# Where the feed-forward's side sums stand: pair 0's sums directly behind their products, w_down's sums two half steps later, the copies of w_down on their own

## The chip, the cores and the metric

The kernel runs on one core of one Trainium2 chip. A core has five engines with a queue of instructions each: TensorE (PE: matmuls, and PEld for the loading of their weights), VectorE (DVE), ScalarE (ACT), GpSimd (POOL) and SyncE (SP, which here only starts DMAs). An engine takes its own instructions strictly in order and waits for others through semaphores. The metric is the device time of one execution in microseconds; lower is better.

## The reference

One layer of a streaming encoder on 1024 tokens of width 1024, float32: token mixing, cross-attention into 256 memory tokens, and a SwiGLU feed-forward (FFN) with a hidden width of 2816. The part that matters here is the last:

```python
def swiglu(h, w_gate, w_up, w_down):
    return (jax.nn.silu(h @ w_gate) * (h @ w_up)) @ w_down
...
        h = rms_norm(x, ffn_pre_g)
        x = x + rms_norm(swiglu(h, w_gate, w_up, w_down), ffn_post_g)
```

## The kernel before

Every product is made of three matmuls, in a split form: an operand `x` is kept as a rounded part (`hi`, by ScalarE, line 113) and a remainder (`lo`, by VectorE, line 115), and `hi*hi + hi*lo + lo*hi` is accumulated in PSUM.

The FFN multiplies blocks by a scheme of Strassen's kind, with seven products in place of eight. The hidden width is cut into 22 tiles of 128, taken as 11 **pairs** (`NPAIR`), and each pair has two **half steps**: m = 0 for w_gate, m = 1 for w_up. A half step is written (pair, m) below. In each:

- `operands(i, m)` (line 1405 on) loads the pair's two weight tiles (L1409), makes the sums S1 to S4 of their blocks (L1417 on GpSimd; L1415 on VectorE for the first), and splits six or seven operands (`op`). `made[0]` remembers the last of GpSimd's sums. It is called one half step ahead.
- `gate_up(i, m, ...)` issues the seven products (each 12 matmuls, `product`, L1314) into four banks of PSUM: `p1`, S4, S3, `p2`, T2, T4, T1. Bank 1 and bank 3 are used twice: ScalarE copies what the first product left (`keep`, L1330) before TensorE adds the second. `add` (L1335) is VectorE's addition of a bank to a copy; the first one in a half step makes `u2`. What is in `held` is issued behind `u2`.
- `sums` makes the four result blocks, c11, c21, c12 and `p7` (L1335, L1460). For m = 0 ScalarE puts Silu on each (L1466). For m = 1 `finish_hid` multiplies the blocks with them (L1357) and stores three of the four to `hs_d` (L1362), a tensor in DRAM. Then, for every pair but pair 0, `hid_sums(i)` makes four more sums of the finished blocks, S3, S1, S2 and S4 (L1372, VectorE), and stores them too.

Pair 0 is special. Its w_gate half is done by eight plain products, and its w_up half, (0, 1), is written out by hand between `operands(0, 1, dve)` and `sums(0, 1, ...)`. Its `hid_sums(0)` is not called there: it is put into `held` of the next half step, (1, 0), behind `u2` and that half step's held operands.

The second matrix, w_down, is needed in blocks and in sums of blocks, too. `wd_sums(k)`, for k = 0 to 21, does two things for half of pair k // 2: it copies one or two blocks of w_down from DRAM to DRAM (`wd_d`, L1380; each behind a certain read of `x1` in the cross-attention, by `issue_after`), and it loads the blocks into the one buffer `wt` (L1383), makes four sums in place on GpSimd (L1387) and stores them to `wt_d` (L1388). The GpSimd part is put behind `made[0]`. It is called at the end of each half step, and twice more at the end.

Then seven **down** products (`DOWN`) read chunks of two pairs from `hs_d` and `wd_d` or `wt_d` into buffers `slab` (L1527, L1529), split them and multiply (L1608). The first takes "11" and `wd_d`, the second S2 and `wt_d`. There are 16 `slab` buffers, which the FFN's own operands occupy first.

The order in each queue is not the order of the text. A planner simulates the kernel when it is built and takes, for each engine, the instruction that is ready in its simulated time and stands earliest in the text; `issue_after(x)` adds an order behind `x` on the same engine. Buffers of a pool are handed on as they come free: 13 for `ev`, 10 for `op`, 1 for `wt`.

Of the kernel before, what the change touches and what calls it, by code (L numbers as in the profile page):

```python
# [52 lines left out]
def layer(ctx: ExitStack, tc: tile.TileContext, a, out):  # L53
# [15 lines left out]
    def slab(shape, dt=F32R):  # L69
        return slabp.tile(shape, dt, name="slab", tag="slab")  # L70
# [1239 lines left out]
    def product(ps, w, name, first):  # L1310
        (wh, wl), (bh, bl) = w, hB[name]
        for k in range(4):
            for n, (x, y) in enumerate(((wh, bh), (wh, bl), (wl, bh))):
                pe.matmul(ps, x[:, k], y[:, k], start=first and k + n == 0, stop=k == 3 and n == 2,  # L1314
                          skip_group_check=not first)
# [28 lines left out]
    def ev():  # L1344
        return evp.tile([P, 512], F32, name="ev", tag="ev")

    def plain_product(f, t):
        ps = (g_ps if t else x_ps)([P, 512])
        for n, name in enumerate((("11", "21"), ("12", "22"))[t]):
            product(ps, plain[0, f][n], name, n == 0)  # L1350
        hid[f, t] = ev()
        with tc.issue_after(tail[0].ins):
            act.activation(out=hid[f, t], in_=ps, func=AF.Silu)

    def finish_hid(i, f, t, u):
        h = hid[f, t]
        dve.tensor_tensor(out=h, in0=u, in1=h, op=ALU.mult)  # L1357
        if (f, t) != (0, 1):
            hid_store(i, "%d%d" % (t + 1, f + 1), h)

    def hid_store(i, name, t):
        stC.dma_start(out=hs_d[HID.index(name), i], in_=t)  # L1362

    def hid_sums(i):

        a11, a12, a21, a22 = hid.pop((0, 0)), hid.pop((1, 0)), hid.pop((0, 1)), hid.pop((1, 1))
        t = {}
        for name, x, y, fn in (("S3", a11, a21, ALU.subtract), ("S1", a21, a22, ALU.add),
                               ("S2", "S1", a11, ALU.subtract), ("S4", a12, "S2", ALU.subtract)):
            t[name] = ev()  # L1370
            x, y = (t[v] if isinstance(v, str) else v for v in (x, y))
            dve.tensor_tensor(out=t[name], in0=x, in1=y, op=fn)  # L1372
            hid_store(i, name, t[name])

    def wd_sums(k):

        p, cs = k // 2, slice(k % 2 * 256, k % 2 * 256 + 256)
        for f, h in ((0, 0), (1, 0), (1, 1))[2 * (k % 2):2 + k % 2]:
            with tc.issue_after(x1_read[min(3 + k // 4, 7)].ins):
                sp.dma_start(out=wd_d[f, h, p], in_=a["w_down"][2 * p + f][:, h * 512:h * 512 + 512])  # L1380
        w = wtp.tile([P, 2, 2, 256], F32, name="wt", tag="wt")
        for f in range(2):
            sp.dma_start(out=w[:, f], in_=a["w_down"][2 * p + f].rearrange("p (h c) -> p h c", c=512)[:, :, cs])  # L1383
        b11, b12, b21, b22 = w[:, 0, 0], w[:, 0, 1], w[:, 1, 0], w[:, 1, 1]
        with tc.issue_after(made[0].ins) if made[0] else ExitStack():
            for o, x, y in ((b11, b12, b11), (b12, b22, b12), (b22, b22, b11), (b21, b21, b22)):
                pool.tensor_tensor(out=o, in0=x, in1=y, op=ALU.subtract)  # L1387
            stC.dma_start(out=wt_d[p, :, :, :, cs], in_=w)  # L1388
# [11 lines left out]
    def op(src):  # L1400
        o = opp.tile([P, 2, 4, P], F32R, name="op", tag="op")
        split(o[:, 0], o[:, 1], src)
        return o[:, 0], o[:, 1]

    def operands(i, m, engine=None, held=None):

        rw = slab([P, 2, KT, P], F32)
        for f in range(2):
            sp.dma_start(out=rw[:, f].rearrange("p k f -> p (k f)"), in_=a[GU[m]][2 * i + f])  # L1409
        a11, a12, a21, a22 = rw[:, 0, 0:4], rw[:, 0, 4:8], rw[:, 1, 0:4], rw[:, 1, 4:8]  # L1410
        s2, s3, s4 = (ssp.tile([P, 4, P], F32, name="ss", tag="ss") for _ in range(3))
        s1 = a21
        def sub(o, x, y, fn=ALU.subtract):
            if engine:
                engine.tensor_tensor(out=o, in0=x, in1=y, op=fn)  # L1415
            else:
                made[0] = pool.tensor_tensor(out=o, in0=x, in1=y, op=fn)  # L1417
        o = {"11": op(a11)} if i else {}
        sub(s3, a11, a21)
        if held is None:  # L1420
            o["S3"] = op(s3)
        sub(s1, a21, a22, ALU.add)
        sub(s2, s1, a11)
        sub(s4, a12, s2)

        def rest():
            if held is not None:
                o["S3"] = op(s3)
            o["S4"] = op(s4)
            if i:  # L1430
                o["12"] = op(a12)
            o["S2"] = op(s2)
            o["22"] = op(a22)
            o["S1"] = op(s1)
        if held is None:
            rest()
        else:
            held.append(rest)
        return o

    def gate_up(i, m, w, q, held=()):
        q.p1(w["11"])
        p1 = q.keep(1)
        product(q.bank(4), w["S4"], "22", True)
        product(q.bank(3), w["S3"], "T3", True)
        p7 = q.keep(3)
        q.p2(w["12"])
        product(q.bank(2), w["S2"], "T2", True)
        u2 = q.add(2, p1)
        with tc.issue_after(q.added.ins) if held else ExitStack():  # L1450
            for part in held:
                part()
        product(q.bank(3), w["22"], "T4", False)
        product(q.bank(2), w["S1"], "T1", False)
        sums(i, m, q, p1, p7, u2, q.b[1])

    def sums(i, m, q, p1, p7, u2, c11):
        c21 = q.add(3, u2, False)
        u4 = q.add(2, p1, False)
        dve.tensor_tensor(out=p7, in0=u4, in1=p7, op=ALU.add)  # L1460
        c12 = q.add(4, u4, False)
        c = {(0, 0): c11, (0, 1): c12, (1, 0): c21, (1, 1): p7}
        if m == 0:
            for k, t in c.items():
                hid[k] = ev() if k == (0, 0) else t
                act.activation(out=hid[k], in_=t, func=AF.Silu)  # L1466
        else:
            for (f, t), u in c.items():
                finish_hid(i, f, t, u)
            if i:  # L1470
                hid_sums(i)

    seq = [(i, m) for i in range(1, NPAIR) for m in range(2)]
    ws = {}
# [4 lines left out]
    second = x_ps([P, 512])  # L1479
    product(second, plain[1, 0][1], "21", True)  # L1480
    w = operands(0, 1, dve)
    for f in range(2):
        plain_product(f, 1)
    hslab("T1")
# [11 lines left out]
    product(first.bank(3), w["22"], "T4", False)  # L1496
    product(first.bank(2), w["S1"], "T1", False)
    sums(0, 1, first, p1, p7, u2, c11)
    for n, (i, m) in enumerate(seq):
        held = []  # L1500
        if n + 1 < len(seq):
            ws[seq[n + 1]] = operands(*seq[n + 1], held=None if n else held)
        if n == 0:
            held.append(lambda: hid_sums(0))
        gate_up(i, m, ws.pop((i, m)), Products(i, m), held)
        wd_sums(n)
    for n in (len(seq), len(seq) + 1):
        wd_sums(n)


# [169 lines left out]
```

## Time and profile before

| | |
|---|---|
| time, median of 3 runs (lowest to highest) | 1403.26 us (1400.19 to 1403.65) |
| the profiled execution: time / span of its instructions | 1402.2 us / 1400.3 us |
| mean granted clock of TensorE | 0.997 |
| busy: PE, DVE, ACT, POOL | 1372.8, 966.4, 648.3, 376.6 us |
| GpSimd's sums of w_down (L1387) | 88 instructions, 83.5 us, 949 ns each |
| loads of `wt` / stores to `wt_d` / copies to `wd_d` | 44 / 22 / 33 DMAs |

The profile is of one execution. A line of a timeline gives the start in us, the length in us, the engine, the line of the kernel, the operation, what is written and read, and how many like it are merged; in brackets stands the idle time before it and what ended it. L113, L115, L1330 and the like are lines of helpers, so many places share them. In the table of stretches "1.00" in the column of the clock is full speed.

### The profile page before, as it was taken

The page shows a single profiled execution, that of the slowest core. Times are in us where ns is not written, and L with a number is a line of the kernel's source. Part 1 is how long each engine was busy: PE and PEld are TensorE (multiplying, and loading weights), DVE is VectorE, ACT ScalarE, POOL GpSimd, SP SyncE. Part 2 cuts the span into 40 slices and gives each one's busy share as a digit, 9 for nine tenths or more (in the row PEclk, how much of TensorE's full clock was granted, in tenths as well). Part 3 has the DMA queues.
Part 4 walks back from the last instruction along what each step waited for, and adds up shares of the span by engine and source line. Part 5 has one row for each costly group of instructions (what it writes and reads, how often), then busy time and mean ns, then how long its engine had stood idle before and what let it go on. Part 6 is the DMA issues. An engine that isn't in the chain of part 4 may idle for free.

```text
span 1400.3 us, 19903 instructions
## 1 busy us (share of the span) xinstructions
PE 1372.8 (98%) x7157; PEld 1144.3 (82%) x7157; DVE 966.4 (69%) x1740; ACT 648.3 (46%) x1264; POOL 376.6 (27%) x430
## 2 busy tenths in 40 slices
PE   9999999999999999999999989999999999999997
PEld 6889898779977787888887768888888888888886
DVE  7959955867758677445567987876777675655566
ACT  7373345875557646443345523333333334544351
POOL 0011110011110251001211556676666663000021
PEclk9999999999999999999999999999999999999999
DMA  6425765468653773044556443554444448955544
GB/s 218 142 104 165 216 226 136 104 179 253 179 160 108 207 242 106 0 155 131 165 183 231 150 153 118 203 174 161 165 142 158 152 150 283 376 196 195 180 166 165
DMA packets 104482, 241.51 MB, mean 172 GB/s; under 512 B 11512, under 2 KB 40184, under 8 KB 104192
## 3 DMA queue, kind: packets, MB, share of 16 engines
q1 hardware_dynamic: 85856, 178.34, 40.7%
q0 software_dynamic: 18528, 61.91, 12.3%
q8 instruction: 56, 0.92, 0.3%
q14 instruction: 42, 0.34, 0.1%
HBM read 171.53 MB, written 79.43 MB: 179 GB/s over the span
## 4 chain that ended last, share of the span: by engine, by line
PE 58%; DVE 2%; issue 1%; ACT 1%; DVEq 0%; ACTq 0%
PE x L1314 16%; PE g L1314 12%; PE x L1608 7%; PE g L1608 7%; PE g L124 2%; PE g L122 2%; PE g L123 2%; PE x L123 2%; PE x L124 2%; PE x L122 2%; PE g L1110 1%; DVE op L115 1%; PE g L1221 0%; DVE ev L1460 0%; DVE ev L1372 0%
## 5 line engine op out<-in xcount | busy, mean ns | idle before, releaser
L1314 PE MATMUL x<-slab,op 128*128 128x512 f32 x984 | 236.4, 392 | 5.9 <-ACT ev L1330 5.6
L1314 PEld LDWEIGHTS x<-slab,op 128*128 128x128 f32 x984 | 185.8, 189 | 46.3 <-ACT ev L1330 6.7
L1314 PE MATMUL g<-slab,op 128*128 128x512 f32 x756 | 181.9, 389 | 0.2 <-ACT op L113 0.2
L115 DVE TENSOR_TENSOR slab<-slab 128x1024 fp32r<-128x1024 f32 (+2 forms) x96 | 115.4, 1208 | 83.4 <-ACT slab L113 81.1
L1314 PEld LDWEIGHTS g<-slab,op 128*128 128x128 f32 x756 | 141.8, 188 | 30.1 <-ACT op L113 0.8
L122 PE MATMUL g<-slab,whl 128*128 128x512 f32 (+1 forms) x416 | 151.5, 364 | 0.8 <-ACT slab L488 0.4
L123 PE MATMUL g<-slab,whl 128*128 128x512 f32 (+1 forms) x416 | 148.4, 357 | 0.0
L124 PE MATMUL g<-slab,whl 128*128 128x512 f32 (+1 forms) x416 | 148.3, 357 | 0.0
L113 ACT ACTIVATE slab<-slab 128x1024 fp32r<-128x1024 f32 (+2 forms) x96 | 99.2, 1038 | 105.6 <-DMA slab<-hs_d 81.0
L1608 PE MATMUL g<-slab 128*128 128x512 f32 x462 | 126.7, 389 | 0.0
L1608 PE MATMUL x<-slab 128*128 128x512 f32 x462 | 126.7, 389 | 0.0
L115 DVE TENSOR_TENSOR op<-slab,op 128x512 fp32r<-128x512 f32 x82 | 95.4, 1175 | 10.6 <-ACT op L113 10.4
L1608 PEld LDWEIGHTS g<-slab 128*128 128x128 f32 x462 | 86.7, 188 | 18.0
L1608 PEld LDWEIGHTS x<-slab 128*128 128x128 f32 x462 | 86.7, 188 | 18.0
L1387 POOL TENSOR_TENSOR wt<-wt 128x256 f32<-128x256 f32 x88 | 83.5, 949 | 30.0 <-DMA wt<-in_w_down 26.6
L122 PEld LDWEIGHTS g<-slab,whl 128*128 128x128 f32 x416 | 78.6, 189 | 12.0 <-ACT whl L113 0.6
L124 PEld LDWEIGHTS g<-slab,whl 128*128 128x128 f32 x416 | 78.4, 189 | 11.6 <-DVE whl L115 0.2
L123 PEld LDWEIGHTS g<-slab,whl 128*128 128x128 f32 x416 | 78.6, 189 | 10.6
L113 ACT ACTIVATE op<-slab 128x512 fp32r<-128x512 f32 x82 | 51.0, 627 | 76.5 <-PE x L1314 37.8
L113 ACT ACTIVATE op<-ss 128x512 fp32r<-128x512 f32 x63 | 39.6, 630 | 99.6 <-PE g L1314 51.5
L115 DVE TENSOR_TENSOR whl<-raw,whl 128x1024 fp32r<-128x1024 f32 (+2 forms) x58 | 64.8, 1124 | 21.5 <-ACT whl L113 21.1
L1417 POOL TENSOR_TENSOR ss<-slab 128x512 f32<-128x512 f32 x40 | 60.4, 1510 | 71.1 <-DVE op L115 32.3
(402 smaller groups left out, 2871.0 us busy)
## 6 DMA issues: line engine op xcount, KB each, us to landing
hs_d<-ev POOLq DMA_DIRECT2D x77, 256.0 KB, 2.7
slab<-hs_d SPq DMA_DIRECT2D x35, 512.0 KB, 10.8
slab<-in_w_up SPq DMA_DIRECT2D x22, 512.0 KB, 5.8
wt<-in_w_down SPq DMA_DIRECT2D x44, 256.0 KB, 3.4
wt_d<-wt POOLq DMA_DIRECT2D x22, 512.0 KB, 5.1
slab<-in_w_gate SPq DMA_DIRECT2D x20, 512.0 KB, 4.9
slab<-wt_d SPq DMA_DIRECT2D x20, 512.0 KB, 5.1
wd_d<-in_w_down SPq DMA_DIRECT2D x33, 256.0 KB, 5.4
```

What stands on the lines that cost most here:

```text
L113: first = act.activation(out=hi, in_=src, func=AF.Copy, scale=1.0 if mul is None else mul)
L115: (lo_eng or dve).tensor_tensor(out=lo, in0=src, in1=hi.bitcast(F32), op=ALU.subtract)
L122: pe.matmul(ps, lh, rh, start=first, stop=False)
L123: pe.matmul(ps, lh, rl, start=False, stop=False)
L124: pe.matmul(ps, ll, rh, start=False, stop=last)
L1110: pe.transpose(tp[:, k], src[:, (k0 + k) * P:(k0 + k + 1) * P], ident)
L1314: pe.matmul(ps, x[:, k], y[:, k], start=first and k + n == 0, stop=k == 3 and n == 2, skip_group_check=not first)
L1387: pool.tensor_tensor(out=o, in0=x, in1=y, op=ALU.subtract)
L1417: made[0] = pool.tensor_tensor(out=o, in0=x, in1=y, op=fn)
L1608: pe.matmul(banks[n][j], xo[:, u, js], wo[:, v], start=ends[0] and k == 0, stop=ends[1] and k == 2, skip_group_check=onto is not None)
```

## The change

It has three parts. `hid_sums(0)` is called in `sums(0, 1, ...)` behind `finish_hid`, as for every other pair, and no longer from `held` of (1, 0). The copies to `wd_d` become a function of their own, `wd_copy(k)`, whose calls stand two half steps earlier than before in the text. What is left of `wd_sums(k)` is called two half steps later: k = 0 behind (2, 0), and the last four calls behind the last half step, where two stood.

```diff
-    def wd_sums(k):
-
-        p, cs = k // 2, slice(k % 2 * 256, k % 2 * 256 + 256)
+    def wd_copy(k):
+        p = k // 2
         for f, h in ((0, 0), (1, 0), (1, 1))[2 * (k % 2):2 + k % 2]:
             with tc.issue_after(x1_read[min(3 + k // 4, 7)].ins):
                 sp.dma_start(out=wd_d[f, h, p], in_=a["w_down"][2 * p + f][:, h * 512:h * 512 + 512])
+
+    def wd_sums(k):
+        p, cs = k // 2, slice(k % 2 * 256, k % 2 * 256 + 256)
         w = wtp.tile([P, 2, 2, 256], F32, name="wt", tag="wt")
...
             for (f, t), u in c.items():
                 finish_hid(i, f, t, u)
-            if i:
-                hid_sums(i)
+            hid_sums(i)
...
     w = operands(0, 1, dve)
+    wd_copy(0)
...
     sums(0, 1, first, p1, p7, u2, c11)
+    wd_copy(1)
     for n, (i, m) in enumerate(seq):
         held = []
         if n + 1 < len(seq):
             ws[seq[n + 1]] = operands(*seq[n + 1], held=None if n else held)
-        if n == 0:
-            held.append(lambda: hid_sums(0))
         gate_up(i, m, ws.pop((i, m)), Products(i, m), held)
-        wd_sums(n)
-    for n in (len(seq), len(seq) + 1):
+        wd_copy(n + 2)
+        if n > 1:
+            wd_sums(n - 2)
+    for n in range(len(seq) - 2, len(seq) + 2):
         wd_sums(n)
```

## The prediction, made before the result was known

> **What bounds the kernel now.** I read the page's head first, then busy time by stretch, then the waits of TensorE.
>
> ```profile
> span 1400.3 us, 19903 instructions
> PE 1372.8 (98%) x7157; PEld 1144.3 (82%) x7157; DVE 966.4 (69%) x1740; ACT 648.3 (46%) x1264; POOL 376.6 (27%) x430
> ```
>
> ```profile
> 820.00:830.00 10.00, 7.65 (x33) 5.69 (x31) 10.00 (x7) 3.16 (x6) 7.20 (x9) 1.00 0.30 117
> 830.00:840.00 10.00, 6.76 (x20) 5.40 (x21) 7.43 (x12) 3.93 (x7) 2.30 (x3) 0.66 0.53 187
> ...
> 860.00:880.00 20.00, 20.00 (x90) 16.56 (x89) 13.81 (x16) 7.26 (x13) 11.35 (x10) 1.00 0.33 115
> ```
>
> ```profile
> 900.00:1000.00 100.00, 100.00 (x443) 82.81 (x442) 70.44 (x87) 34.24 (x58) 67.54 (x67) 1.00 0.51 173
> ```
>
> TensorE (PE) is busy for 98% of the span, and in the later stretches of the FFN shown here for all of it. So what the change makes lighter on other engines counts only where TensorE stands still. The columns are the stretch and its length, then PE, weight loads, DVE, ACT, POOL, the granted clock and DMA. In 820 to 840 us TensorE lacks 5.6 us, VectorE (DVE) is full at first, and the clock falls to 0.66. The waits (total, times, longest) and TensorE's timeline (start, length) name the place:
>
> ```profile
> PE x L1314 <- ACT ev L1330: 5.6, 2, 5.3
> ```
>
> ```profile
> 823.13 3.02 PE L1314 MATMUL x<-slab,op 128*128 128x512 f32 x12 [0.30 <-ACT ev L1330]
> ...
> 827.57 0.39 PE L1314 MATMUL x<-slab,op 128*128 128x512 f32 x1
> 833.24 7.43 PE L1314 MATMUL x<-slab,op 128*128 128x512 f32 x22 [5.28 <-ACT ev L1330]
> ...
> 873.38 5.38 PE L1314 MATMUL x<-slab,op 128*128 128x512 f32 x23
> ```
>
> Both waits are for ScalarE (ACT) in the second half step of pair 1, called (1,1): line 1330 is `keep`, which copies a bank of PSUM that TensorE then adds onto. Why that copy is late stands in the chain of waits (start, us on the chain, what) and in ScalarE's timeline:
>
> ```profile
> 815.78 1.20 DVE ev L1372 x2
> ...
> 821.00 0.60 DVE ev L1372
> ...
> 822.21 2.80 DVE ev L1372
> ...
> 825.61 4.71 DVE ev L1460
> ...
> 830.85 0.69 DVE ev L1335
> ```
>
> ```profile
> 830.36 0.63 ACT L1466 ACTIVATE ev<-ev 128x512 f32<-128x512 f32 x1 [6.76 <-DVE ev L1460]
> 831.56 0.63 ACT L1466 ACTIVATE ev<-ev 128x512 f32<-128x512 f32 x1 [0.57 <-DVE ev L1335]
> ...
> 832.61 0.58 ACT L1330 ACTIVATE ev<-x 128x512 f32<-128x512 f32 x1
> ```
>
> The copy at 832.61 stands in ScalarE's queue behind two Silus (L1466) of half step (1,0), and these wait for VectorE's additions L1460 and L1335. VectorE is late for two reasons, and the change takes up both. First, the four sums of pair 0 (L1372, `hid_sums(0)`) stand in that queue. Second, single instructions are stretched:
>
> ```profile
> L1372 DVE TENSOR_TENSOR ev<-ev x44: 676/1103/2877, 815.7 to 1202.7; 128x512 f32<-128x512 f32 x44
> ```
>
> ```profile
> L1460 DVE TENSOR_TENSOR ev<-ev x21: 679/693/4787, 800.2 to 1190.9; 128x512 f32<-128x512 f32 x21
> ```
>
> ```profile
> L1335 DVE TENSOR_TENSOR ev<-x,ev x21: 677/691/692, 797.7 to 1185.9; 128x512 f32<-128x512 f32 x21
> ```
>
> ```profile
> 825.88 0.75 POOL L1387 TENSOR_TENSOR wt<-wt 128x256 f32<-128x256 f32 x1
> ...
> 828.51 1.25 POOL L1417 TENSOR_TENSOR ss<-slab 128x512 f32<-128x512 f32 x1
> ```
>
> With one operand in PSUM an addition of this size never takes over 0.69 us (the three numbers are minimum, median and maximum in ns); with both in SBUF it takes up to 4.79. That longest one, on the chain from 825.61 to 830.32, ends just after an unbroken row of four GpSimd (POOL) sums, of which the first and the last are shown, ending at 829.76. Two of the four are sums of w_down (L1387), two are operand sums (L1417). The Trainium skill, "SBUF — State Buffer", section "SBUF: two separate sides", says that a VectorE operation with two SBUF inputs and a GpSimd operation exclude each other for a whole instruction; these rows agree.
>
> **The change part by part.** *The sums of pair 0* move to the end of `sums(0, 1)`. What VectorE and GpSimd do there:
>
> ```profile
> 801.49 1.83 DVE L1357 TENSOR_TENSOR ev<-ev 128x512 f32<-128x512 f32 x2
> 808.19 0.69 DVE L1335 TENSOR_TENSOR ev<-g,ev 128x512 f32<-128x512 f32 x1 [4.86 <-issue]
> ```
>
> ```profile
> 809.62 1.61 POOL L1417 TENSOR_TENSOR ss<-slab 128x512 f32<-128x512 f32 x1 [4.07 <-DVE op L115]
> ...
> 816.68 0.56 POOL L1362 DMA_DIRECT2D hs_d<-ev  x1 [2.05 <-DVE ev L1372]
> ```
>
> After the last products of pair 0 are finished (L1357, until 803.32) VectorE is idle for 4.86 us. Four sums at the unstretched minimum need 2.7 us; at twice the median (2.2 us each) 8.8 us. I take 2.7, as GpSimd is idle itself for 4.07 us before 809.62, so nothing much stretches them. Were it 8.8, VectorE's next instruction (`u2` of (1,0), at 808.19) would come 3.9 us late; TensorE adds onto that bank after one more product of 2.7 us, so the price is at most 1.2 us. The four stores to `hs_d` go along: 0.56 us each, 2.2 together, in GpSimd's same gap. Where they stood, GpSimd's queue waited for VectorE (2.05 us at the first) with operand sums behind; that goes. The buffers (`ev`) are freed earlier, not later.
>
> *The sums of w_down* start behind (2,0), so no L1387 stands before some 833 us. I put both parts through the chain. Without L1372 (1.20, 0.60 and 2.80 us out) and with L1460 at 0.60 instead of 4.71, the L1335 of 830.85 starts at 830.85 - 4.60 - 4.11 = 822.1. From there to the end of `keep` (833.19) it takes 2.34 us, so `keep` ends near 824.5. TensorE needs it when the matmul at 827.57 has gone in, a step of 0.23 later, at 827.8. So the wait is gone with 3.3 us to spare. If GpSimd's operand sums alone still stretched L1460 as today, `keep` would end at 828.6 and 0.8 us of wait would stay: that is the first part's worth alone, at the least. The second part alone (L1372 stays, but 2.20 shorter at 822.21, and L1460 4.11 shorter) ends `keep` near 826.9, also in time.
>
> What goes with the wait: 5.28 + 0.30 us of idle, and the slow clock behind it. 23 matmuls take 5.38 us at 873.38, a step of 0.227 and 0.39 for one, so 22 take 5.16; at 833.24 they took 7.43, that is 2.27 more; the 12 at 823.13 took 0.13 more than 2.89. **Sum: 5.58 + 2.27 + 0.13 = 8.0 us.** The Trainium skill, "TensorE: Matmul & The Clock Gate", section "What's actually happening", has the clock halved after an idle window of about 3.4 us, until it has been busy as long; by that the clock's part would be an estimated 1.7 us and the sum 7.4.
>
> What is late next? From (2,0) on the sums of w_down and the operand sums meet VectorE as they do today one pair later:
>
> ```profile
> 866.00 1.77 DVE L1460 TENSOR_TENSOR ev<-ev 128x512 f32<-128x512 f32 x1
> ```
>
> ```profile
> 870.62 0.57 ACT L1330 ACTIVATE ev<-x 128x512 f32<-128x512 f32 x1
> ```
>
> GpSimd is busy for 11.35 of 20 us there, L1460 takes 1.77 us, and `keep` still ends at 871.19, 2.2 us before the matmuls at 873.38 that I take to be its user. No wait.
>
> *The copies to `wd_d`* on SyncE's queue (SP) are emitted earlier and apart:
>
> ```profile
> 699.86 6.42 SPq L1380 DMA_DIRECT2D wd_d<-in_w_down x9
> ```
>
> These are the last 9 of 33; every group follows a read of x1 that `issue_after` names, and the change leaves those names as they are. So they stay where they are, at 0. If some slipped into the FFN, each would take 0.71 us of SP's queue (6.42 / 9), beside a TensorE that is fed; I bound that by 0 and 2 us.
>
> *At the end* six calls of `wd_sums` instead of four come behind the last operand sums:
>
> ```profile
> 1136.53 3.90 POOL L1387 TENSOR_TENSOR wt<-wt 128x256 f32<-128x256 f32 x4
> ...
> 1172.53 0.73 POOL L1387 TENSOR_TENSOR wt<-wt 128x256 f32<-128x256 f32 x1 [5.86 <-DMA wt<-in_w_down]
> ...
> 1176.50 0.74 POOL L1388 DMA_DIRECT2D wt_d<-wt  x1 [0.30 <-POOL wt L1387]
> ```
>
> ```profile
> 1169.35 1.20 SPq L1383 DMA_DIRECT2D wt<-in_w_down x2
> ...
> 1175.26 0.36 SPq L1527 DMA_DIRECT2D slab<-hs_d  x1
> ...
> 1185.44 0.33 SPq L1527 DMA_DIRECT2D slab<-hs_d  x1
> ...
> 1208.33 0.47 SPq L1529 DMA_DIRECT2D slab<-wt_d  x1
> ```
>
> ```profile
> 1181.53 0.84 PE L1608 MATMUL x<-slab 128*128 128x512 f32 x3
> ...
> 1186.47 1.22 DVE L115 TENSOR_TENSOR slab<-slab 128x1024 fp32r<-128x1024 f32 x1
> ```
>
> The four calls follow each other by 12.0 us ((1172.53 - 1136.53) / 3), since there is one `wt` buffer: load, four sums, store, and only then the next load. Two more put the last store at 1200.5. Its reader goes out at 1208.33 today and serves the last pair of the second down product, some 1239 us. So the data are in time. But the load of the last call (1169.35 today) then waits on SP's queue until 1193.4, and loads of down operands may stand behind it. The first down product starts at 1181.53 and takes 2.72 us a pair (twelve matmuls), with one product of 2.72 between; pair 8 is needed at 1206.0, pair 10 at 1211.5. Their loads go out at 1175.26 and 1185.44 today. Behind the late load one goes out at 1194.6 and is split by 1207.0 (12.4 us, as from 1175.26 to 1187.69). That covers pair 10 and misses pair 8 by 1.0 us. I take 0, as the planner has pair 8's load two calls earlier; the other end is the third rival.
>
> **The rivals.** *Part of it stays* (0.17): the planner that orders the queues places things anew, and a `keep`, a Silu or a down operand comes 1 to 5 us late beside the gain of 8.0. For it: margins of only 3.3, 2.2 and -1.0 us. Against it: a TensorE without any wait in the later stretches. Time 1396.5 to 1401, say 1398.5.
>
> *The wait moves* (0.14): the sums of w_down begin at (2,0) and pile up there as they did in (1,0); or the planner puts pair 0's sums where they were, so that the change does not do what it says. For it: GpSimd and VectorE have as much work as before. Against it: the rows at 866.00 and 870.62. Then the 8.0 us come back: 1403.3. The skill's rule on the shared port, named above, speaks for this rival, as the change lowers no number of exclusions.
>
> *The tail turns the sign* (0.07): SP stands at the wait for `wt` ahead of pair 8's loads. This costs from a release at 1192.4 on, a us of idle for each us; with 2.3 us of slow clock on top it eats the gain of 8.0 at a release at 1198.1, and beyond that the kernel is slower. If GpSimd's calls, against a busy VectorE, come 14.5 us apart instead of 12.0 (six of them: 15 us later, 1208.4), the wait is 16.0 us and the time 1395.3 + 16.0 + 2.3 = 1413.6. Against it: it needs both, the order and the longer calls.
>
> **How the numbers follow.** The profiled execution took 1402.2 us around its span of 1400.3; less 8.0 that is 1394.2. The median shown, 1403.26, lies 1.06 above it, so beside the median the forecast is 1395.3, with a chance of 0.62. About 0.3% (4.2 us) is what a measurement of this kernel can tell from no change. Faster takes the forecast's 0.62 and half of the first rival: 0.71. Same: the other half and the second rival: 0.22. Slower: 0.07. The range runs from 1392.0 (runs of before go 3.1 us below their median, to 1400.19) to 1401.0, the end of the first rival; the other two, 0.21, stay out. The bounds of 1.2 us for `u2` and 2 us for the copies lie within it.
>
> **What would show it.** Right: no wait of TensorE on L1330 in (1,1), a clock of 1.00 from 820 to 840 us, L1372 first at about 803 us, no L1387 before 830, the down projection starting near 1173.5. Wrong: a new wait over 1 us on `keep` in (2,0) or (2,1), L1372 still behind 810, or TensorE waiting for a split of a down operand between 1195 and 1210.

## The result, and the profile after

| | before | after |
|---|---|---|
| time, median (lowest to highest) | 1403.45 us (1400.19 to 1409.21), 6 runs | 1394.68 us (1392.73 to 1397.30), 6 runs |
| ratio of the times, 95% interval | | 0.9931 (0.9916 to 0.9945) |
| profiled execution: time / span | 1402.2 / 1400.3 us | 1395.97 / 1393.9 us |
| mean granted clock | 0.997 | 0.998 |

The kernel is faster by 8.8 us, more than the 4.2 us that its measurement can tell from no change; forecast were 1395.3 us and a gain of 8.0. In the kernel after, most lines stand two or three further down: L1389 are the sums of w_down (L1387 before), L1390 their stores (L1388), L1419 the operand sums (L1417), L1462 the addition that was stretched (L1460), L1468 the Silus (L1466), L1385 the loads of `wt` (L1383), L1530 and L1532 the loads of down operands (L1527, L1529), L1611 the down products (L1608).

First the busy time by stretch: one row of before that the prediction did not show, and then after (columns as there: the stretch and its length, PE, weight loads, DVE, ACT, POOL, granted clock, DMA).

```profile
799.00:857.00 58.00, 52.41 (x221) 42.54 (x220) 47.44 (x50) 16.44 (x29) 36.51 (x40) 0.94 0.39 138
```

```profile
799.00:857.00 58.00, 58.00 (x257) 48.06 (x256) 44.26 (x53) 20.50 (x36) 38.76 (x39) 1.00 0.40 141
820.00:830.00 10.00, 10.00 (x46) 8.29 (x45) 5.54 (x7) 3.85 (x7) 9.46 (x8) 1.00 0.19 64
830.00:840.00 10.00, 10.00 (x45) 8.28 (x45) 6.26 (x9) 2.42 (x4) 6.51 (x7) 1.00 0.57 198
...
1154.00:1173.00 19.00, 17.89 (x79) 14.53 (x78) 7.55 (x9) 8.43 (x11) 6.64 (x10) 1.00 0.83 277
```

Between 799 and 857 us TensorE was busy for 52.41 us at a clock of 0.94; now it is for all 58, at 1.00, and does 257 matmuls in place of 221. 36 more at a step of 0.227 us are **8.2 us**: the forecast's 8.0 is there. The last row shows something that was not there: 1.1 us of idle at the end of the FFN. So do the waits of TensorE from 780 us on; in place of 5.6 us in two waits there is

```profile
PE x L1314 <- ACT ev L1330: 1.1, 1, 1.1
```

Now the place of the old wait. TensorE after, then VectorE, ScalarE and GpSimd (start, length, what, idle before it):

```profile
824.84 2.88 PE L1314 MATMUL g<-slab,op 128*128 128x512 f32 x12
827.56 5.38 PE L1314 MATMUL x<-slab,op 128*128 128x512 f32 x23
```

```profile
802.50 2.75 DVE L1372 TENSOR_TENSOR ev<-ev 128x512 f32<-128x512 f32 x4
806.07 0.69 DVE L1335 TENSOR_TENSOR ev<-g,ev 128x512 f32<-128x512 f32 x1 [0.83 <-PE g L1314]
...
819.06 0.69 DVE L1462 TENSOR_TENSOR ev<-ev 128x512 f32<-128x512 f32 x1
819.78 0.69 DVE L1335 TENSOR_TENSOR ev<-g,ev 128x512 f32<-128x512 f32 x1
```

```profile
820.84 0.61 ACT L1468 ACTIVATE ev<-ev 128x512 f32<-128x512 f32 x1
...
822.86 0.58 ACT L1330 ACTIVATE ev<-x 128x512 f32<-128x512 f32 x1
```

```profile
824.91 1.30 POOL L1419 TENSOR_TENSOR ss<-slab,ss 128x512 f32<-128x512 f32 x1
826.17 3.96 POOL L1389 TENSOR_TENSOR wt<-wt 128x256 f32<-128x256 f32 x4
```

Pair 0's four sums now stand directly behind the products and take 2.75 us. `u2` (806.07) still waits 0.83 us for TensorE: the sums delay nothing. The addition that took 4.79 us takes 0.69 (819.06), and `keep` ends at 823.44. In before TensorE did one of the 23 matmuls that stand at 827.56 here, and waited at the second. Now it comes to the second at 827.79, so `keep` is 4.3 us early.

And now the new wait. TensorE, ScalarE and SyncE's queue after:

```profile
1167.56 2.88 PE L1314 MATMUL g<-slab,op 128*128 128x512 f32 x12
1170.28 0.61 PE L1611 MATMUL g<-slab 128*128 128x512 f32 x2
1172.01 3.04 PE L1314 MATMUL x<-slab,op 128*128 128x512 f32 x12 [1.11 <-ACT ev L1330]
```

```profile
1170.41 1.06 ACT L113 ACTIVATE slab<-slab 128x1024 fp32r<-128x1024 f32 x1 [4.14 <-DMA slab<-hs_d]
1171.38 0.58 ACT L1330 ACTIVATE ev<-x 128x512 f32<-128x512 f32 x1
```

```profile
1162.51 1.20 SPq L1385 DMA_DIRECT2D wt<-in_w_down  x2
1163.75 0.60 SPq L1530 DMA_DIRECT2D slab<-hs_d  x1
```

The last `keep` of the FFN stands in ScalarE's queue behind the split (L113) of a down operand, and that split waits 4.14 us for its load from `hs_d`. TensorE waits 1.11 us for `keep`. The wait was not absent before by much; the same place in before, TensorE and ScalarE:

```profile
1178.47 3.00 PE L1314 MATMUL x<-slab,op 128*128 128x512 f32 x12
```

```profile
1176.84 1.06 ACT L113 ACTIVATE slab<-slab 128x1024 fp32r<-128x1024 f32 x1 [4.07 <-DMA slab<-hs_d]
1177.80 0.58 ACT L1330 ACTIVATE ev<-x 128x512 f32<-128x512 f32 x1
```

There the same split stood ahead of the same `keep`, which ended at 1178.38, 0.1 us before TensorE came to it.

So the balance in the two profiled executions is: 8.3 us gained in pair 1, 1.3 us given back at the end of the FFN (1.11 of idle, and 12 matmuls in 3.04 instead of 2.88 us), 7.0 us net. The spans differ by 6.4, as the FFN itself stood 0.6 us later after (the matmul from which the next section counts at 799.46 us against 798.86).

### The profile page after: what moved, and what is told of

It is laid out like the page before. It is cut to its first block, busy times and chain, and to the rows that moved or that the text cites. A ratio compares the mean times of both kernels' runs of the same rounds, so it can differ in the third digit from the quotient of the medians.

```text
span 1393.9 us, 19904 instructions
## 1 busy us (share of the span) xinstructions
PE 1371.1 (98%) x7157; PEld 1144.7 (82%) x7157; DVE 955.8 (69%) x1740; ACT 648.7 (47%) x1264; POOL 382.4 (27%) x430
## 4 chain that ended last, share of the span: by engine, by line
PE 56%; DMA 2%; DVE 1%; issue 1%; ACT 1%; POOL 0%; SPq 0%; DVEq 0%; POOLq 0%; ACTq 0%
PE x L1314 15%; PE g L1314 11%; PE x L1611 8%; PE g L1611 7%; PE g L124 2%; PE g L122 2%; PE g L123 2%; PE x L123 2%; PE x L124 2%; PE x L122 2%; PE g L1110 1%; DMA slab<-hs_d 1%; DMA wt_d<-wt 1%; PE g L1221 0%; POOL wt L1389 0%
## 5 line engine op out<-in xcount | busy, mean ns | idle before, releaser
L1314 PE MATMUL x<-slab,op 128*128 128x512 f32 x984 | 233.7, 389 | 1.4 <-ACT ev L1330 1.1
L1314 PEld LDWEIGHTS x<-slab,op 128*128 128x128 f32 x984 | 184.5, 188 | 40.6 <-ACT ev L1330 1.5
L1314 PE MATMUL g<-slab,op 128*128 128x512 f32 x756 | 181.8, 389 | 0.2 <-ACT op L113 0.2
L115 DVE TENSOR_TENSOR slab<-slab 128x1024 fp32r<-128x1024 f32 (+2 forms) x96 | 116.1, 1218 | 86.0 <-ACT slab L113 83.9
L1314 PEld LDWEIGHTS g<-slab,op 128*128 128x128 f32 x756 | 141.8, 188 | 30.1 <-ACT op L113 0.8
L113 ACT ACTIVATE slab<-slab 128x1024 fp32r<-128x1024 f32 (+2 forms) x96 | 98.9, 1037 | 108.4 <-DMA slab<-hs_d 74.6
L1611 PE MATMUL x<-slab 128*128 128x512 f32 x462 | 126.7, 389 | 0.0
L1611 PE MATMUL g<-slab 128*128 128x512 f32 x462 | 126.7, 389 | 0.0
L1611 PEld LDWEIGHTS g<-slab 128*128 128x128 f32 x462 | 86.7, 188 | 18.0
L1611 PEld LDWEIGHTS x<-slab 128*128 128x128 f32 x462 | 86.7, 188 | 18.0
L115 DVE TENSOR_TENSOR op<-slab,op 128x512 fp32r<-128x512 f32 x82 | 91.9, 1134 | 11.1 <-ACT op L113 10.8
L1389 POOL TENSOR_TENSOR wt<-wt 128x256 f32<-128x256 f32 x88 | 85.8, 975 | 24.9 <-DMA wt<-in_w_down 21.0
L113 ACT ACTIVATE op<-slab 128x512 fp32r<-128x512 f32 x82 | 51.3, 628 | 81.5 <-PE x L1314 39.8
L1419 POOL TENSOR_TENSOR ss<-slab 128x512 f32<-128x512 f32 x40 | 63.1, 1577 | 88.3 <-DVE op L115 35.7
L113 ACT ACTIVATE op<-ss 128x512 fp32r<-128x512 f32 x63 | 39.6, 630 | 97.9 <-PE g L1314 50.9
L115 DVE TENSOR_TENSOR whl<-raw,whl 128x1024 fp32r<-128x1024 f32 (+2 forms) x58 | 64.9, 1124 | 22.4 <-ACT whl L113 22.1
```

Source lines behind the costliest of these rows:

```text
L113: first = act.activation(out=hi, in_=src, func=AF.Copy, scale=1.0 if mul is None else mul)
L115: (lo_eng or dve).tensor_tensor(out=lo, in0=src, in1=hi.bitcast(F32), op=ALU.subtract)
L1611: pe.matmul(banks[n][j], xo[:, u, js], wo[:, v], start=ends[0] and k == 0, stop=ends[1] and k == 2, skip_group_check=onto is not None)
```

## Experiments

The time before the FFN scatters: in the profiles of all these kernels the FFN's first matmul starts between 749.6 and 758.8 us, though no kernel differs there in what it computes. So beside each time stands the **FFN interval**, from the start of the 201st matmul of L1314 (the 200th, when the first is number 0, as in the recorded expectations) to the start of the program's last matmul, worked out from the profiled execution. It holds every place to which a sum is moved or from which it goes; the copies go out before the FFN (in after the last of them at 705.6 us).

| kernel | median, us | of before beside it | ratio (95%) | FFN interval | below before |
|---|---|---|---|---|---|
| before | 1403.45 | | | 593.92 | |
| after | 1394.68 | 1403.45 | 0.9931 (0.9916 to 0.9945) | 586.90 | 7.02 |
| e1: only pair 0's sums | 1396.87 | 1404.57 | 0.9946 (0.9928 to 0.9964) | 588.37 | 5.55 |
| e2: only w_down, sums and copies | 1400.16 | 1404.57 | 0.9966 (0.9952 to 0.9979) | 590.27 | 3.65 |
| e3: only the copies | 1404.51 | 1404.57 | 1.0003 (0.9989 to 1.0017) | 593.98 | -0.06 |
| e4: after, sums of w_down caught up | 1393.91 | 1404.57 | 0.9923 (0.9904 to 0.9942) | 587.03 | 6.89 |
| e5: after, last `keep` first | 1395.39 | 1404.37 | 0.9940 (0.9923 to 0.9957) | 585.48 | 8.44 |
| e6: e1, last `keep` first | 1398.00 | 1404.37 | 0.9960 (0.9945 to 0.9975) | 586.17 | 7.75 |
| e7: after, pair 0's sums left out | 1396.38 | 1404.37 | 0.9942 (0.9922 to 0.9963) | 586.58 | 7.34 |
| e8: after, sums of w_down later still | 1401.65 | 1404.37 | 0.9980 (0.9968 to 0.9993) | 592.47 | 1.45 |

The first four test the prediction's split of the gain into parts, and the new wait.

**e1: only pair 0's sums move.** Before, with one edit:

```diff
-            if i:
-                hid_sums(i)
+            hid_sums(i)
...
-        if n == 0:
-            held.append(lambda: hid_sums(0))
```

> The kernel before with pair 0's four sums moved behind their products, and nothing else. Chain theory (VectorE's queue, each part alone nearly enough): TensorE waits at most 0.8 us on keep in (1,1), no slow clock behind it, and the end of the FFN is as before (no wait there), so 1395 to 1396, a ratio of 0.9945. If the wait needs both parts to go (the stretching of VectorE's additions by the sums of w_down is the main cause): L1460 is still stretched to over 3 us in (1,0), a wait of 2 to 5 us stays, 1398 to 1402.

The wait in (1,1) is gone altogether. VectorE, GpSimd and TensorE of e1 (lines as before, L1387 and L1460):

```profile
819.91 0.68 DVE L1460 TENSOR_TENSOR ev<-ev 128x512 f32<-128x512 f32 x1
```

```profile
814.60 3.48 POOL L1387 TENSOR_TENSOR wt<-wt 128x256 f32<-128x256 f32 x3
820.28 1.49 POOL L1417 TENSOR_TENSOR ss<-slab 128x512 f32<-128x512 f32 x1 [2.20 <-DMA slab<-in_w_up]
```

```profile
826.92 5.38 PE L1314 MATMUL x<-slab,op 128*128 128x512 f32 x23
...
1172.82 3.04 PE L1314 MATMUL x<-slab,op 128*128 128x512 f32 x12 [2.57 <-ACT ev L1330]
```

The sums of w_down are still in this half step, yet L1460 takes 0.68 us. With pair 0's sums gone from (1,0), their stores no longer hold GpSimd's queue there (before: 2.05 us at the first of them). GpSimd does three sums of w_down early, at 814.60, is then idle for 2.20 us until the next weights land, and L1460 starts in that gap. No run moved the sums and left their stores behind, so the part of the stores is read from these rows and not tested. At the end of the FFN the new wait is there too, and larger: 2.57 us.

**e2: only the sums and copies of w_down.** After, with `hid_sums(0)` put back into `held`:

```diff
-            hid_sums(i)
+            if i:
+                hid_sums(i)
...
+        if n == 0:
+            held.append(lambda: hid_sums(0))
```

> The changed kernel with pair 0's sums back behind u2 of (1,0): the sums of w_down start two half steps later, the copies stand apart. Chain theory: VectorE's additions are unstretched enough that keep ends near 827 beside a need at 827.8, so the 5.3 us go; the wait of 1.1 us at the end of the FFN that the changed kernel shows stays: 1396 to 1397, a ratio of 0.995. If the four sums in VectorE's queue are the main cause: a wait of 2 to 5 us stays in (1,1), 1398 to 1403.

The wait stays, smaller. TensorE, the chain of waits (start, us on the chain), VectorE behind it and GpSimd of e2:

```profile
834.35 6.73 PE L1314 MATMUL x<-slab,op 128*128 128x512 f32 x22 [3.01 <-ACT ev L1330]
```

```profile
825.46 2.12 DVE ev L1372
827.58 0.60 DVE op L115
828.19 2.14 DVE ev L1462
```

```profile
830.25 1.78 DVE L115 TENSOR_TENSOR op<-slab,op 128x512 fp32r<-128x512 f32 x1
```

```profile
828.46 1.30 POOL L1419 TENSOR_TENSOR slab<-slab 128x512 f32<-128x512 f32 x1
829.84 1.64 POOL L1419 TENSOR_TENSOR ss<-slab 128x512 f32<-128x512 f32 x1
```

No sum of w_down is near, and the two additions still take 2.1 us each on the chain, and the remainder of an operand (L115) behind them takes 1.78 where it took 0.68 in before: GpSimd's operand sums alone stretch them. The other wait that was expected here, 1.1 us at the end of the FFN, is not there: `keep` ends at 1178.57 and TensorE comes to it at 1178.88.

**e3: only the copies.** e2, with the sums of w_down back in their old places as well:

```diff
         wd_copy(n + 2)
-        if n > 1:
-            wd_sums(n - 2)
-    for n in range(len(seq) - 2, len(seq) + 2):
+        wd_sums(n)
+    for n in (len(seq), len(seq) + 1):
         wd_sums(n)
```

> The kernel before with the copies to wd_d apart and earlier in the text, and nothing else. Chain theory: the same waits of 5.3 and 0.3 us on L1330, all copies out by 706 us, 1402 to 1404, a ratio of 1.000. If the copies had a part in the gain: below 1400.

The copies apart are worth nothing: the ratio is 1.0003, and the waits read as before.

```profile
PE x L1314 <- ACT ev L1330: 5.6, 2, 5.3
```

**e4: do the late calls make the new wait?** After, with two calls of `wd_sums` behind two of the half steps, so that only two are left behind the last one, as before:

```diff
+    done = 0
...
         if n > 1:
-            wd_sums(n - 2)
-    for n in range(len(seq) - 2, len(seq) + 2):
+            for _ in range(2 if n in (8, 12) else 1):
+                wd_sums(done)
+                done += 1
+    for n in range(done, len(seq) + 2):
         wd_sums(n)
```

> The changed kernel, but two of w_down's sums are called twice in a half step in the middle (n = 8 and 12), so that four calls instead of six stand behind the last operand sums, as before. Theory that the new wait of 1.1 us at the end of the FFN comes from SyncE standing at the wait for the wt buffer ahead of the down operands: the wait goes, TensorE has no wait after 800 us, about 1 us less than the changed kernel: ratio to before 0.992 to 0.993. If that wait has another cause (the planner's order of ScalarE's queue alone): it stays at 1 us and the time is the changed kernel's. If two calls in one half step pile up on VectorE: a new wait at n = 8 or 12.

TensorE of e4:

```profile
1170.65 3.01 PE L1314 MATMUL x<-slab,op 128*128 128x512 f32 x12 [1.26 <-ACT ev L1330]
```

The wait stays, at 1.26 us. That the sums of w_down run further behind at the end is not its cause, and the idea falls.

**e5 and e6: the last `keep` ahead of the splits.** The second idea: the wait is made in ScalarE's queue, by the split that stands ahead. In e5 (from after) and e6 (from e1) the splits of the first down product's operands from pair 4 on come behind the last `keep`:

```diff
         def keep(self, n):
             t = ev()
-            act.activation(out=t, in_=self.b[n], func=AF.Copy)
+            last_keep[0] = act.activation(out=t, in_=self.b[n], func=AF.Copy)
...
-        split(xo[:, 0], xo[:, 1], xl)
-        split(wo[:, 0], wo[:, 1], wl)
+        with tc.issue_after(last_keep[0].ins) if x == "11" and p >= 4 else ExitStack():
+            split(xo[:, 0], xo[:, 1], xl)
+            split(wo[:, 0], wo[:, 1], wl)
```

> The changed kernel, with the splits of the first down product's operands from pair 4 on put behind the last keep on ScalarE's and no other wait added. Theory: the wait of 1.1 us near the end of the FFN is keep standing behind such a split, which waits for a load that went out late; then it goes, and from the FFN's 200th matmul to the last matmul it takes 585.6 us instead of 586.9: ratio to before 0.992. If keep is late for VectorE or for its own input: 1.1 us stay. If the split behind keep is late in its turn: a new wait on a slab in the down product.

> The same edit on the kernel with pair 0's sums moved and w_down's sums where they were. Theory that the later sums of w_down bring nothing in (1,1) and that the kernel with pair 0's sums alone lost 2.6 us at the end of the FFN only by keep standing behind a split: no wait in (1,1), none at the end, the same 585.6 us as its twin with the whole change, ratio 0.992. If the later sums of w_down do help: this one is 1 us or more slower than its twin.

ScalarE and TensorE of e5:

```profile
1163.79 0.58 ACT L1330 ACTIVATE ev<-x 128x512 f32<-128x512 f32 x1
1167.27 1.06 ACT L113 ACTIVATE slab<-slab 128x1024 fp32r<-128x1024 f32 x1 [2.90 <-DMA slab<-hs_d]
```

```profile
1168.39 2.88 PE L1314 MATMUL x<-slab,op 128*128 128x512 f32 x12
```

The split still waits for its load, but nobody waits for the split: `keep` ends at 1164.37, 4.0 us before it is needed, and the 12 matmuls take 2.88 us again. In e6 the 2.57 us go in the same way; TensorE waits 0.39 us on another addition there:

```profile
1179.30 3.01 PE L1314 MATMUL g<-slab,op 128*128 128x512 f32 x12 [0.39 <-DVE ev L1335]
```

In the FFN interval e5 is 1.4 us below after and e6 is 2.2 below e1. The whole times do not follow: e5's ratio and that of after overlap, and so do e5's and e6's, whose medians lie 2.6 us apart where the FFN explains 0.7. e5 has the shortest span of all profiled executions but cannot be called faster than after. The gain of the medians lies between 1.4 us below that of the FFN interval (e6) and 3.8 above it (e4), and the seven executions of e7 alone spread from 1391.78 to 1402.68 us. What makes the front of the program scatter was not settled.

**e7: what do pair 0's sums cost where they now stand?** After, with a finished block stored in the place of each sum, so that the four stores stay:

```diff
+            if i == 0:
+                hid_store(i, name, a11)
+                continue
             t[name] = ev()
```

> The changed kernel without pair 0's four sums: a block is stored in the place of each, so the stores stay and 4 of VectorE's additions go. If the sums are free where they stand now (in VectorE's idle time behind (0, 1)): 586.9 us from the FFN's 200th matmul to the last, as with them, and the same time within 1 us. If they still cost something there: up to 1.2 us less.

The FFN interval falls by 0.3 us, and TensorE's wait at the end by as much:

```profile
1178.95 3.02 PE L1314 MATMUL x<-slab,op 128*128 128x512 f32 x12 [0.81 <-ACT ev L1330]
```

In pair 1 there is nothing left that the sums cost. They are free where VectorE was idle anyway.

**e8: how far can the sums of w_down be put off?** After, two half steps later again:

```diff
-        if n > 1:
-            wd_sums(n - 2)
-    for n in range(len(seq) - 2, len(seq) + 2):
+        if n > 3:
+            wd_sums(n - 4)
+    for n in range(len(seq) - 4, len(seq) + 2):
         wd_sums(n)
```

> The changed kernel with w_down's sums four half steps later instead of two: eight calls behind the last operand sums instead of six. Tail theory (the calls follow each other by 12 to 15 us, and SyncE stands at the wait for the wt buffer and at the read of the last wt_d ahead of the down operands): the last release comes 25 to 30 us later, past 1215, the last pair's read of the second down product misses its turn near 1231, TensorE waits 5 to 15 us in the second or third down product: 1400 to 1410. If the down operands' lead hides it: as the changed kernel, 1394 to 1396.

TensorE, GpSimd, SyncE's queue and the stretches of e8:

```profile
1237.80 0.79 PE L1611 MATMUL g<-slab 128*128 128x512 f32 x1 [4.00 <-ACT slab L113]
```

```profile
1229.97 0.73 POOL L1390 DMA_DIRECT2D wt_d<-wt  x1 [0.30 <-POOL wt L1389]
```

```profile
1233.35 0.33 SPq L1532 DMA_DIRECT2D slab<-wt_d  x1
```

```profile
1225.00:1235.00 10.00, 8.80 (x39) 6.94 (x37) 0.00 (x0) 0.00 (x0) 3.68 (x5) 1.00 0.34 113
1235.00:1245.00 10.00, 7.20 (x20) 5.68 (x21) 5.51 (x7) 5.45 (x6) 0.00 (x0) 0.66 0.94 340
```

The last store of the sums goes out at 1229.97, the read of them in the second down product at 1233.35, and TensorE stands for 4.0 us; the clock falls to 0.66 behind it. The interval is 592.47, 5.6 us above after (6.8 against an after without its own 1.3 of wait and restart), so that most of the gain is gone. In after, the last load of `wt` and that same read:

```profile
1193.48 1.86 SPq L1385 DMA_DIRECT2D wt<-in_w_down  x2
...
1215.19 0.32 SPq L1532 DMA_DIRECT2D slab<-wt_d  x1
```

The read goes out 18.2 us earlier than in e8, for a TensorE that comes to it at about the same time, so some 14 us are to spare.

## Why the prediction was right, point by point

**What bounds the kernel** held. The gain came where TensorE had stood still: the 5.6 us of idle went, and with it the slow clock behind it. Counted by matmuls the gain in pair 1 is 8.2 us, by starts 8.3, forecast 8.0. The trace's own 2.27 us for the clock was a good term. By the Trainium skill, "TensorE: Matmul & The Clock Gate", section "What's actually happening", the sum would have been an estimated 7.4.

**The cost of the moved sums** held: 2.75 us at 802.50 (forecast 2.7 at about 803), and `u2` undelayed. e7 bounds what they cost by 0.3 us.

**The chain to `keep`** held with a margin of 4.3 us instead of 3.3: the addition L1335 came at 819.78 (forecast 822.1), `keep` ended at 823.44 (824.5).

**The split into parts failed once, and was too careful once.** The step that failed is the one by which the second part alone ends `keep` near 826.9, "also in time": it took 2.20 us off L1372 and set L1460 to 0.60 once no sum of w_down was near. They took 2.12 and 2.14 (e2), since the operand sums suffice to stretch them, and L115 behind them 1.10 more than in before. Together these 4.2 us ate the forecast's 0.9 us of spare, and 3.0 us of wait stayed. The bound on the first part, 0.8 us of wait left, kept L1460's stretch where L1372 was gone. But the stores of the same sums had held up GpSimd's queue; without them GpSimd's own work moved too, and e1 has no wait there. By the starts of TensorE's matmuls e1 gains 8.3 us in pair 1, as much as the whole change. So pair 0's sums carry the whole gain in (1,1), and w_down's sums two half steps later add nothing there that e1 has not. At the end of the FFN they may help: after waits 1.1 us where e1 waits 2.6. With that wait out of the way in both, 0.7 us remain between e5 and e6.

**The copies at 0** held (e3: 1.0003).

**What is late next** was looked for in the wrong place. (2,0) and (2,1) have no wait, as forecast. But the list of things that could come late next stopped at (2,1) and at the down operands, and left out the last `keep`, whose row in before has a margin of 0.1 us. This is the first rival ("a `keep`, a Silu or a down operand comes 1 to 5 us late beside the gain") in its mildest form, 1.1 us, and it stands together with the forecast rather than against it. Why the margin went can be followed in GpSimd's and SyncE's rows. GpSimd's store ahead of this place, before:

```profile
1165.92 0.74 POOL L1388 DMA_DIRECT2D wt_d<-wt  x1 [0.30 <-POOL wt L1387]
```

SyncE, before (the `wt` load ahead of it goes out at 1169.35):

```profile
1170.59 0.60 SPq L1527 DMA_DIRECT2D slab<-hs_d  x1
```

GpSimd's, after:

```profile
1158.15 0.74 POOL L1390 DMA_DIRECT2D wt_d<-wt  x1 [0.30 <-POOL wt L1389]
```

The load from `hs_d` stands in SyncE's queue behind the next load of `wt`, and that waits until the store of the sums has landed. Before, store to `wt` load took 3.43 us and `hs_d` load to split 6.25. After it was 4.36 (1158.15 to 1162.51) and 6.66 (1163.75 to 1170.41), 1.34 us more. TensorE came 12.55 us after the store before (1178.47) and would have come 12.75 after it now (1172.01 less the wait). So 0.1 of margin and 0.2 more, less 1.34, make -1.0, and 1.11 us were waited. e5 shows that the place in ScalarE's queue decides; why the two transfers landed later, with no more traffic (a DMA share of 0.83 from 1154 to 1173, and of 0.86 from 1162 to 1181 in before), was not settled, and no run took the `wt` load out of SyncE's way. The wait is a matter of tenths: e2 and e8, whose sums of w_down are as late as in after or later, do not have it, while e1, e4 and e7 do.

**The third rival** has its mechanism in e8, two calls later than the change puts it: sums of w_down that come too late for the down products. In after nothing was lost in this way, but not for the reason of the forecast's 12.0 us a call. GpSimd's last call and SyncE's load for pair 8, after:

```profile
1203.57 5.05 POOL L1389 TENSOR_TENSOR wt<-wt 128x256 f32<-128x256 f32 x4 [4.84 <-DMA wt<-in_w_down]
```

```profile
1167.53 0.36 SPq L1530 DMA_DIRECT2D slab<-hs_d  x1
```

The six calls came 14.9 us apart ((1203.57 - 1129.01) / 5), so the longer calls that the rival asks for, 14.5, were there. That the last `wt` load went out at 1193.48, beside the forecast's 1193.4, is luck: the forecast counts in the times of before, and the down products come 6.4 us earlier in after (1175.11 in place of 1181.53), so that the like of it would be 1187.0. What held is the order: pair 8's load stands two calls ahead, at 1167.53. SyncE then stood before the read at 1215.19 without TensorE noticing. In e8 the place was another: it lost its time at the last read of `wt_d` in the second product, which waits for the data, and not at pair 8's loads in the first.

**The tests named beforehand**: clock 1.00 and no wait, met; sums at 803, met; "no L1387 before 830", missed, they began at 826.17 without harm; the down projection near 1173.5 was 1175.11 (for the three matmuls that stood at 1181.53), later by the 1.3 us of the new wait and the 0.6 of the FFN's later start, less the 0.3 more gained in pair 1.

**The size.** The profiled executions differ by 6.2 us and the medians by 8.8. The FFN explains 7.0: the forecast's 8.0 and 0.3 more in pair 1, less the 1.3 of the wait that it did not see. The remaining 1.8 us of the medians lies within the scatter of the front and is not claimed for the change, so that the median came within 0.7 us of the forecast is in part luck. (By the forecast's own working its range would begin at 1392.2, not at 1392.0.)

## What to carry to other kernels

When an engine with a queue in order is late for the one copy that TensorE waits for, move its side work directly behind that work's own inputs, into time in which the engine is idle anyway: here that was the whole gain, and thinning the work on the neighbouring engine alone left over half of the wait. Side work that stores its results also holds up the queue that issues the stores, so count both queues. And when a wait in the middle is to go, look through all later copies of the same kind for those that were in time by a few tenths of a us, and at what stands ahead of them in their queue.

## What the runs showed of the hardware

**How long one idle of TensorE is does not settle whether the slow clock follows.** These are idle times of TensorE in the FFN, one occurrence each, in front of a group of matmuls, and what the group took beyond its length without idle (12 matmuls 2.88 us, 22 matmuls 5.16):

| idle, us | where | beyond its length, us |
|---|---|---|
| 0.81 | e7, end of the FFN | 0.14 (12) |
| 1.11 | after, end of the FFN | 0.16 (12) |
| 1.26 | e4, end of the FFN | 0.13 (12) |
| 2.57 | e1, end of the FFN | 0.16 (12) |
| 3.01 | e2, (1,1) | 1.57 (22) |
| 5.28 | before, (1,1) | 2.27 (22) |

Among these rows, up to 2.57 us the idle costs itself and 0.13 to 0.16 us; 3.01 us costs 1.6 us on top, and 5.28 us 2.3. But this is no threshold, for ahead of the FFN shorter idles had the slow clock behind them. TensorE of e6 there, and the stretch behind the idle (the last columns are the granted clock and DMA):

```profile
395.50 0.50 PE L736 MATMUL s<-slab,a 128*128 128x512 f32 x1 [2.23 <-DVE nlr L743]
```

```profile
395.60:399.00 3.40, 3.40 (x12) 2.83 (x13) 2.92 (x9) 2.42 (x6) 0.54 (x1) 0.55 0.73 231
```

Behind 2.23 us of idle the clock was 0.55 there, and behind 2.52 us in e2 (at 396.36) it was 0.63 from 396.4 to 401; behind 2.57 us in e1 (at 1172.82) it was 1.00. What decides beside the length was not settled. The Trainium skill, "TensorE: Matmul & The Clock Gate", section "What's actually happening", gives an idle window of about 3.4 us; here 3.01 us, and once 2.23 us, were enough.

**One VectorE operation can be held across several of GpSimd's.** The 4.79 us of L1460 in before are more than any single GpSimd operation beside it (0.72 to 1.30 us), and it ends 0.56 us behind the last of four GpSimd sums in an unbroken row (at 829.76). In e2 one operand sum of 1.30 us (828.46 to 829.76) is enough to hold the same addition: it stands on the chain from 828.19 to 830.33. Additions with an operand in PSUM (L1335) took at most 0.69 us in every run.
